# Two rings instead of one: separate buffers for modulation tiles and mixer weights

## The chip, the cores and the metric

The kernel runs on one core of a Trainium2 chip. The metric is the device time of one execution in microseconds; lower is better. The core has a matrix engine (PE), a vector engine (DVE), a scalar engine (ACT), a general engine (POOL), and SP, whose queue here only issues DMAs. Every engine takes its own queue strictly in order; engines meet through semaphores.

## The reference

One decoder layer, 256 tokens, width 2048, all in float32. Six modulation vectors come from the conditioning vector `c`; the token mixer sums a block-attention branch and a gated DeltaNet branch; then a SwiGLU feed-forward part.

```python
mod = silu(c) @ w_ada + b_ada                       # 2048 x 12288: 96 columns of 128
sh1, sc1, g1, sh2, sc2, g2 = split(mod, 6)
h = x * (1 + sc1) + sh1
proj = h @ w_in                                     # q,k,v | conv q,k,v | z | b,a | gate_a, gate_b
y_a = moba_attention(qa, ka, va)                    # 8 heads of 128
o = gated_delta_rule(l2norm(q), l2norm(k), v, ...)  # 16 heads, chunks of 64, triangular solve
y_b = rmsnorm(o) * silu(z)
y = (sigmoid(gate_a) * (y_a @ w_proj_moba) + sigmoid(gate_b) * (y_b @ w_proj_gdn)) @ w_out
x = layer_norm(ALPHA * x + g1 * y)
x = layer_norm(ALPHA * x + g2 * swiglu(x * (1 + sc2) + sh2))
```

## The kernel before

**Steps.** All large products run as 572 steps. A step loads one weight tile of up to 128 x 1024 float32 (512 KB, tile `raw`, SP issues its DMA, `load_w`, line 204), and splits it in two: ACT rounds it to `hi` (line 211), DVE computes the remainder `lo = raw - hi` (line 212). PE then multiplies in three passes (hi by activation hi, hi by activation lo, lo by activation hi): 24 matmuls of 256 columns a step (lines 289 to 291), or 12 of 512 columns (lines 337 to 339), or a wide form in the feed-forward part (lines 296 and 300). `hi` and `lo` have four buffers each. `run(3)` starts the load of a step three steps ahead.

**Modulation sums.** A column of `silu(c) @ w_ada` is not worked out on PE: a tile of w_ada lies with the 128 outputs of the column on the partitions, and one DVE instruction multiplies it with `cb` (silu of c, the same on all partitions) and adds along the row (`ada_sum`, line 229). In the opening 40 whole columns (1 MB each, tiles `r`) are summed. The other 56 columns are summed in halves of 512 KB, the tiles `raw_a` (DMA at line 240): 80 halves in the mixer and 32 in the feed-forward part. A sum leaves two rows in a listing of the queue, the multiply-and-reduce and a short read of its result.

**Buffers.** In the kernel before, `raw` and `raw_a` share one ring of four buffers of 128 x 1024, in the pool `wp`: a load waits until the tile four before it has been read.

**Background work.** After the matmuls of a step, `tick()` lets four background lanes go on (`moba`, `main`, `pre`, `ada`, in this order) for a budget of 1.8 us a step. The lanes are written as generators that yield the cost of what they did. The lane `ada` holds the modulation sums; after each sum it rests for `pace["gap"]` steps. The order in which instructions then stand in each engine's queue is set by a scheduler of the framework, with its own estimates: it can pull an instruction ahead of where the code has it. So a number of steps in `pace` is not the distance in the queue.

**Stages.** Steps 0 to 99 are the opening (first modulation vectors, first columns of w_in); 100 to 131 the attention's and the DeltaNet's q, k, v; 132 to 179 gate_a and w_proj_moba; 180 to 211 z; 212 to 243 gate_b; 244 to 275 w_proj_gdn; 276 to 307 w_out; from 308 the feed-forward part (176 steps in, 88 out).

**Block inverse.** For each of two groups of eight heads (b = 0, 1) the DeltaNet lane inverts blocks of 32 x 32 on DVE (`Ub`), copies the transpose to `mt` (line 669), and sends both through DRAM (`ubd`, POOL, lines 670 and 671) back into the tiles `UU` and `TT` (line 678). PE multiplies with `TT` into `ps` (line 691), DVE scales that to `z` (lines 700, 712), and so on; these chains stand in the same queues as the steps. In the kernel after most of these lines stand 7 higher, and 8 to 14 higher from about line 860 on.

Of the kernel before, what the change touches and what calls it, by code (L numbers as in the profile page):

```python
# [10 lines left out]
F32 = mybir.dt.float32  # L11
# [7 lines left out]
P = 128  # L19
D = 2048  # L20
S = 256
KT = D // P
# [70 lines left out]
def layer(ctx, tc, a, out):  # L93
# [57 lines left out]
    hold = {x: 0 for x in bg}  # L151
    pace = {"all": 1.8, "gap": 1, "debt": 0.0}
    done = set()
# [12 lines left out]
    def tick():  # L166
        for x in hold:
            hold[x] = max(0, hold[x] - 1)
        pace["debt"] = min(pace["debt"] + pace["all"], 2 * pace["all"])
        while pace["debt"] > 0:  # L170
            for lane in ("moba", "main", "pre", "ada"):
                c = advance(lane) if hold[lane] == 0 else None
                if c is None:
                    continue
                if c < 0:
                    hold[lane] = -c
                    continue
                pace["debt"] -= c
                if lane == "ada":
                    hold[lane] = pace["gap"]  # L180
                break
            else:
                return
# [13 lines left out]
    def until(flag):  # L197
        while flag not in done:
            yield rest()

    def load_w(w, k0, kn, c0, cn):
        raw = wp.tile([P, 1024], F32, tag="raw", name="raw", bufs=4)
        v = raw[:, :kn * cn].rearrange("p (k n) -> p k n", n=cn)
        dma.dma_start(raw[:, :kn * cn], w.tile(k0, kn, c0, cn))
        return v
# [27 lines left out]
    def ada_sums(order, ahead):  # L233
        todo = [(col, half) for col in order for half in range(2)]
        held = []
        for n in range(len(todo) + ahead):
            if n < len(todo):
                col, half = todo[n]
                raw = wp.tile([P, 1024], F32, tag="raw", name="raw_a", bufs=4)
                dma.dma_start(raw, w_ada.tile(8 * half, 8, col * P, P, by_column=True))  # L240
                held.append((col, half, raw))
            if n >= ahead:
                ada_sum(*held.pop(0), 2)
                yield 1.35
# [615 lines left out]

    def begin():
        ya = perm.tile([P, 2, MH, S], F32R, tag="s2", name="ya")
        for x in range(2):
# [7 lines left out]
    cur = {}  # L871
# [113 lines left out]
    for j in range(4, 8):  # L985
        ws_unit(ybT, w_pg, 256 * j, KT, merge(j))

    def bcast_row(v, dst):
        ps = pt.tile([P, 512], F32, tag="tp", name="tpr")
        t_.transpose(ps[:KT, :P], adac[:, 16 * v:16 * v + 16], ident)  # L990
        rw = wp.tile([KT, P], F32, tag="acc", name="rw", bufs=2)
        v_.tensor_copy(rw, ps[:KT, :P])
# [14 lines left out]
    def resid(ps, c0, cn, gb, base, dst, st, n):  # L1007
        cc = slice(c0, c0 + cn)
        for h in range(2):
            t = wp.tile([P, 512], F32, tag="acc", name="rt", bufs=2)[:, :cn]  # L1010
            v_.tensor_tensor(t, ps[h], gb[:, cc], op=OP.mult)
# [47 lines left out]

    def ffn_begin():  # L1060
        halves = [perm.tile([P, 8, 2, S], F32R, tag=tag, name="h2") for tag in ("s0", "s1")]
        cur["h2"] = halves
# [16 lines left out]
    def norm2(g):  # L1079
        r, mv, rs = cur["r"], cur["mv"], cur["rs"]  # L1080
        for f in range(4 * g, 4 * g + 4, 2):
# [4 lines left out]
            tp = pt.tile([P, 2, S], F32, tag="tp", name="tp")  # L1086
            hf = wp.tile([P, 2, S], F32, tag="acc", name="hf2", bufs=2)
            for i in range(2):
# [51 lines left out]
    def ln1_affine():  # L1140
        r = cur["r"]
        for n in range(4):
            cc = slice(512 * n, 512 * n + 512)
            for v, op in (("ln1_g", OP.mult), ("ln1_b", OP.add)):
                lg = wp.tile([P, 512], F32, tag="acc", name="lg", bufs=2)
                dma.dma_start(lg, a[v][0, cc].partition_broadcast(P))
# [4 lines left out]
    def ffn_more():  # L1151
# [3 lines left out]
        bg["ada"].append(ada_sums(range(5 * KT, 6 * KT), 1))  # L1155
        pace["gap"] = 4

# [86 lines left out]
```

## Time and profile before

| | |
|---|---|
| median of 3 runs (lowest, highest) | 1789.39 us (1779.66, 1791.91) |
| the profiled execution: its time, its span | 1785.36 us, 1783.6 us |
| PE busy | 1686.6 us (95%) |
| DVE busy | 1249.9 us (70%) |
| ACT busy | 815.2 us (46%) |
| mean granted clock of PE | 0.983 |

PE is busy 95% of the span. A busy share is an average over stages: the rows below show the stages apart.

### The profile page before, as it was taken

The page shows a single profiled execution, that of the slowest core. Times are in us where ns is not written, and L with a number is a line of the kernel's source. Part 1 is how long each engine was busy: PE and PEld are TensorE (multiplying, and loading weights), DVE is VectorE, ACT ScalarE, POOL GpSimd, SP SyncE. Part 2 cuts the span into 40 slices and gives each one's busy share as a digit, 9 for nine tenths or more (in the row PEclk, how much of TensorE's full clock was granted, in tenths as well). Part 3 has the DMA queues.
Part 4 walks back from the last instruction along what each step waited for, and adds up shares of the span by engine and source line. Part 5 has one row for each costly group of instructions (what it writes and reads, how often), then busy time and mean ns, then how long its engine had stood idle before and what let it go on. Part 6 is the DMA issues. An engine that isn't in the chain of part 4 may idle for free.

```text
span 1783.6 us, 28261 instructions
## 1 busy us (share of the span) xinstructions
PE 1686.6 (95%) x11149; PEld 1537.1 (86%) x11149; DVE 1249.9 (70%) x1786; ACT 815.2 (46%) x1118; POOL 49.9 (3%) x68
## 2 busy tenths in 40 slices
PE   3899999999989999899999899999999999999995
PEld 3899999979989788889998899888888888888895
DVE  6899988888856787657875677676666655455454
ACT  3544445667433445336344344544444444433342
POOL 0000000110100001000000000000000000000001
PEclk9999999999999999999999999999999999999998
DMA  9999887666677577876876647777777755765652
GB/s 356 331 339 353 345 310 227 199 196 189 205 238 238 186 237 247 271 239 206 296 265 222 191 129 245 251 252 239 238 246 232 242 193 192 258 197 188 197 185 82
DMA packets 115158, 421.56 MB, mean 236 GB/s; under 512 B 13456, under 2 KB 14384, under 8 KB 109392
## 3 DMA queue, kind: packets, MB, share of 16 engines
q1 hardware_dynamic: 110016, 402.21, 66.7%
q0 software_dynamic: 5008, 17.53, 3.7%
q8 instruction: 88, 1.44, 0.3%
q14 instruction: 46, 0.38, 0.1%
HBM read 412.27 MB, written 7.42 MB: 235 GB/s over the span
## 4 chain that ended last, share of the span: by engine, by line
PE 41%; issue 15%; DMA 8%; DVE 5%; ACT 1%; POOL 0%; POOLq 0%; DVEq 0%; ACTq 0%
PE mm L296 16%; PE mm L300 8%; DMA raw_a<-in_w_ada 4%; DVE lo L212 3%; PE mm L290 3%; PE mm L291 3%; PE mm L289 3%; PE mm L339 2%; PE mm L338 2%; PE mm L337 2%; DMA raw<-in_w_proj_gdn 2%; DMA raw<-in_w_in 1%; ACT hi L211 1%; PE ps L691 1%; DMA rb<-rnd 1%
## 5 line engine op out<-in xcount | busy, mean ns | idle before, releaser
L211 ACT CAST hi<-raw 128x1024 fp32r<-128x1024 f32 (+2 forms) x572 | 582.0, 1020 | 768.7 <-PE mm L339 210.7
L212 DVE TENSOR_TENSOR lo<-raw,hi 128x1024 fp32r<-128x1024 f32 (+2 forms) x572 | 672.8, 1183 | 286.1 <-ACT hi L211 282.1
L289 PE MATMUL mm<-s,hi 128*128 128x256 f32 x1184 | 338.9, 286 | 4.9 <-ACT hi L211 4.7
L291 PE MATMUL mm<-s,lo 128*128 128x256 f32 x1184 | 333.3, 283 | 6.3 <-DVE lo L212 6.2
L290 PE MATMUL mm<-s,hi 128*128 128x256 f32 x1184 | 332.5, 281 | 0.0
L296 PE MATMUL mm<-h,hi 128*128 128x512 f32 x1280 | 319.0, 391 | 0.0
L296 PEld LDWEIGHTS mm<-h,hi 128*128 128x128 f32 x1280 | 228.8, 188 | 39.5
L289 PEld LDWEIGHTS mm<-s,hi 128*128 128x128 f32 x1184 | 225.0, 190 | 10.8 <-ACT hi L211 7.5
L291 PEld LDWEIGHTS mm<-s,lo 128*128 128x128 f32 x1184 | 224.2, 190 | 9.4 <-DVE lo L212 8.5
L290 PEld LDWEIGHTS mm<-s,hi 128*128 128x128 f32 x1184 | 224.8, 190 | 0.4
L300 PEld LDWEIGHTS mm<-h,lo 128*128 128x128 f32 x1280 | 171.1, 188 | 13.2
L300 PE MATMUL mm<-h,lo 128*128 128x256 f32 x1280 | 174.1, 278 | 0.0
L337 PE MATMUL mm<-hi,ach 128*128 128x512 f32 (+1 forms) x440 | 152.6, 347 | 0.0
L338 PE MATMUL mm<-lo,ach 128*128 128x512 f32 (+1 forms) x440 | 152.5, 347 | 0.0
L339 PE MATMUL mm<-hi,acl 128*128 128x512 f32 (+1 forms) x440 | 152.5, 347 | 0.0
L229 DVE CUSTOM_DVE_ANT_0 raw_a<-raw_a,cb,cols 128x1024 f32<-128x1024 f32 x56 | 71.8, 1283 | 77.9 <-DMA raw_a<-in_w_ada 77.9
L229 DVE CUSTOM_DVE_ANT_0 raw_a<-raw_a,cb,ada_half 128x1024 f32<-128x1024 f32 x56 | 71.8, 1283 | 64.8 <-DMA raw_a<-in_w_ada 64.8
L229 DVE CUSTOM_DVE_ANT_0 r<-r,cb,cols 128x2048 f32<-128x2048 f32 x40 | 93.7, 2347 | 14.1 <-DMA r<-in_w_ada 14.1
L337 PEld LDWEIGHTS mm<-hi,ach 128*128 128x128 f32 x440 | 83.3, 189 | 10.4
L339 PEld LDWEIGHTS mm<-hi,acl 128*128 128x128 f32 x440 | 83.3, 189 | 10.4
L338 PEld LDWEIGHTS mm<-lo,ach 128*128 128x128 f32 x440 | 83.3, 189 | 10.1
L338 PE MATMUL mm<-lo,s 128*128 128x512 f32 x192 | 77.0, 401 | 2.2 <-DVE lo L212 2.2
(288 smaller groups left out, 2383.2 us busy)
## 6 DMA issues: line engine op xcount, KB each, us to landing
raw<-in_w_ffn_in SPq DMA_DIRECT2D x176, 512.0 KB, 4.3
raw<-in_w_in SPq DMA_DIRECT2D x168, 512.0 KB, 4.4
raw_a<-in_w_ada SPq DMA_DIRECT2D x112, 512.0 KB, 4.5
raw<-in_w_ffn_out SPq DMA_DIRECT2D x88, 512.0 KB, 4.3
r<-in_w_ada SPq DMA_DIRECT2D x40, 1024.0 KB, 7.6
raw<-in_w_proj_gdn SPq DMA_DIRECT2D x32, 512.0 KB, 4.5
raw<-in_w_out SPq DMA_DIRECT2D x32, 512.0 KB, 4.2
raw<-in_w_in SPq DMA_DIRECT2D x40, 384.0 KB, 5.8
```

Of the source, the lines that this page charges most:

```text
L211: s_.copy(hi, raw)
L212: v_.tensor_tensor(lo, raw, hi.bitcast(F32), op=OP.subtract)
L229: v_.tensor_tensor_reduce(out=raw, in0=raw, in1=cb[:, n * part:n * part + n], scale=1.0, scalar=cols[:, col:col + 1] if first else h, op0= ...
L289: t_.matmul(o, hi[:, i, c], ah, start=(first and i == 0 and t == 0), stop=False)
L290: t_.matmul(o, hi[:, i, c], al, start=False, stop=False)
L291: t_.matmul(o, lo[:, i, c], ah, start=False, stop=(last and i == kn - 1 and t == 1))
L296: t_.matmul(box[t].rearrange("p (u i) -> p u i", u=2), hi[:, i, t * P:(t + 1) * P], both[k0 + i], start=(first and i == 0), stop=False)
L300: t_.matmul(box[t][:, :S], lo[:, i, t * P:(t + 1) * P], both[k0 + i][:, 0, :], start=False, stop=(last and i == kn - 1))
L337: t_.matmul(box[h], xh, hi[:, i, :], start=start, stop=False)
L338: t_.matmul(box[h], xh, lo[:, i, :], start=False, stop=False)
L339: t_.matmul(box[h], xl, hi[:, i, :], start=False, stop=stop)
L691: t_.matmul(ps[:lt.shape[1], n, :], lt, rt, start=True, stop=True)
```

## The change

The diff does four things. The ring of four becomes a ring of three (`raw`) and a ring of two (`raw_a`). `load_w` takes the ring of two for two of every five weight tiles (`turn["n"] % 5 in (1, 3)`) while `turn["both"]` holds, which is in the opening and from the start of the feed-forward part; in the mixer (from `begin()` to `ffn_begin()`) weights use only the ring of three, and the ring of two holds modulation tiles alone. The rest of lane `ada` after a sum becomes 2 steps while the lanes `main` or `pre` have work, 1 otherwise, 4 in the feed-forward part as before. And small tiles (`rw`, `rt`, `hf2`, `lg`) move from pool `wp` to other pools, which makes room for the fifth buffer.

```diff
--- before.py
+++ after.py
@@ -149,7 +149,7 @@
 
     bg = {"moba": [], "main": [], "pre": [], "ada": []}
     hold = {x: 0 for x in bg}
-    pace = {"all": 1.8, "gap": 1, "debt": 0.0}
+    pace = {"all": 1.8, "gap": 2, "free": 1, "debt": 0.0}
     done = set()
 
     def advance(lane):
@@ -177,7 +177,7 @@
                     continue
                 pace["debt"] -= c
                 if lane == "ada":
-                    hold[lane] = pace["gap"]
+                    hold[lane] = pace["gap" if bg["main"] or bg["pre"] else "free"]
                 break
             else:
                 return
@@ -198,8 +198,15 @@
         while flag not in done:
             yield rest()
 
+    turn = {"n": 0, "both": True}
+
+    def raw_a(nm):
+        return wp.tile([P, 1024], F32, tag="raw_a", name=nm, bufs=2)
+
     def load_w(w, k0, kn, c0, cn):
-        raw = wp.tile([P, 1024], F32, tag="raw", name="raw", bufs=4)
+        turn["n"] += 1
+        second = turn["both"] and turn["n"] % 5 in (1, 3)
+        raw = raw_a("raw2") if second else wp.tile([P, 1024], F32, tag="raw", name="raw", bufs=3)
         v = raw[:, :kn * cn].rearrange("p (k n) -> p k n", n=cn)
         dma.dma_start(raw[:, :kn * cn], w.tile(k0, kn, c0, cn))
         return v
@@ -236,7 +243,7 @@
         for n in range(len(todo) + ahead):
             if n < len(todo):
                 col, half = todo[n]
-                raw = wp.tile([P, 1024], F32, tag="raw", name="raw_a", bufs=4)
+                raw = raw_a("raw_a")
                 dma.dma_start(raw, w_ada.tile(8 * half, 8, col * P, P, by_column=True))
                 held.append((col, half, raw))
             if n >= ahead:
@@ -859,6 +866,7 @@
             yield 0.7
 
     def begin():
+        turn["both"] = False
         ya = perm.tile([P, 2, MH, S], F32R, tag="s2", name="ya")
         for x in range(2):
             ya_ops[x].extend(ya[:, x, k, :] for k in range(MH))
@@ -985,10 +993,15 @@
     for j in range(4, 8):
         ws_unit(ybT, w_pg, 256 * j, KT, merge(j))
 
+    def acc(nm, shape):
+        if "k3" in cur:
+            return cur["k3"].tile(shape, F32, tag="acc", name=nm, bufs=2)
+        return c2(nm, shape)
+
     def bcast_row(v, dst):
         ps = pt.tile([P, 512], F32, tag="tp", name="tpr")
         t_.transpose(ps[:KT, :P], adac[:, 16 * v:16 * v + 16], ident)
-        rw = wp.tile([KT, P], F32, tag="acc", name="rw", bufs=2)
+        rw = acc("rw", [KT, P])
         v_.tensor_copy(rw, ps[:KT, :P])
         rd = dr.tile([KT, P], F32, name=f"rd{v}")
         sdma.dma_start(rd, rw)
@@ -1007,7 +1020,7 @@
     def resid(ps, c0, cn, gb, base, dst, st, n):
         cc = slice(c0, c0 + cn)
         for h in range(2):
-            t = wp.tile([P, 512], F32, tag="acc", name="rt", bufs=2)[:, :cn]
+            t = acc("rt", [P, 512])[:, :cn]
             v_.tensor_tensor(t, ps[h], gb[:, cc], op=OP.mult)
             v_.scalar_tensor_tensor(dst[:, h, cc], base[:, h, :], ALPHA, t, op0=OP.mult, op1=OP.add)
             v_.bn_stats(st[:, h, n, :], dst[:, h, cc])
@@ -1058,6 +1071,7 @@
     pss, h2 = [], []
 
     def ffn_begin():
+        turn["both"] = True
         halves = [perm.tile([P, 8, 2, S], F32R, tag=tag, name="h2") for tag in ("s0", "s1")]
         cur["h2"] = halves
         for k in range(KT):
@@ -1084,7 +1098,7 @@
                 tc.keep_in_program_order(v_.tensor_scalar(r[:, h, cc], r[:, h, cc], mv[:, h, 0:1], rs[:, h],
                                                           op0=OP.subtract, op1=OP.mult))
             tp = pt.tile([P, 2, S], F32, tag="tp", name="tp")
-            hf = wp.tile([P, 2, S], F32, tag="acc", name="hf2", bufs=2)
+            hf = acc("hf2", [P, 2, S])
             for i in range(2):
                 for h in range(2):
                     t_.transpose(tp[:, i, h * P:(h + 1) * P], r[:, h, (f + i) * P:(f + i + 1) * P], ident)
@@ -1142,7 +1156,7 @@
         for n in range(4):
             cc = slice(512 * n, 512 * n + 512)
             for v, op in (("ln1_g", OP.mult), ("ln1_b", OP.add)):
-                lg = wp.tile([P, 512], F32, tag="acc", name="lg", bufs=2)
+                lg = acc("lg", [P, 512])
                 dma.dma_start(lg, a[v][0, cc].partition_broadcast(P))
                 for h in range(2):
                     v_.tensor_tensor(r[:, h, cc], r[:, h, cc], lg, op=op)
@@ -1153,7 +1167,7 @@
         act(1, pairs_of(pss[2]), pairs_of(pss[3]))
         bg["main"].append(ln1_affine())
         bg["ada"].append(ada_sums(range(5 * KT, 6 * KT), 1))
-        pace["gap"] = 4
+        pace["gap"] = pace["free"] = 4
 
     do(ffn_more)
```

The scheduler changes the order of the queues with it. Counted against the `lo` of the weight steps, the 80 sums of the mixer stand in the queue of DVE as follows. Before: 10 in steps 100 to 159, 24 in 160 to 215, 46 in 216 to 275. After: 26, 54 and none. In steps 170 to 179 there were 10 and are 20.

SP's queue in the stage of gate_a and w_proj_moba, before: a modulation tile and a weight tile take turns.

```order
L204 DMA raw<-in_w_in 128x1024
L240 DMA raw_a<-in_w_ada 128x1024
L204 DMA raw<-in_w_in 128x1024
L240 DMA raw_a<-in_w_ada 128x1024
L204 DMA raw<-in_w_in 128x1024
L240 DMA raw_a<-in_w_ada 128x1024
L204 DMA raw<-in_w_in 128x1024
L240 DMA raw_a<-in_w_ada 128x1024
L204 DMA raw<-in_w_proj_moba 128x1024
L240 DMA raw_a<-in_w_ada 128x1024
```

The same place after.

```order
L211 DMA raw<-in_w_proj_moba 128x1024 x2
L247 DMA raw_a<-in_w_ada 128x1024 x2
L211 DMA raw<-in_w_in 128x1024
L247 DMA raw_a<-in_w_ada 128x1024 x7
L211 DMA raw<-in_w_in 128x1024
L247 DMA raw_a<-in_w_ada 128x1024
L211 DMA raw<-in_w_in 128x1024 x2
L247 DMA raw_a<-in_w_ada 128x1024 x2
L211 DMA raw<-in_w_proj_moba 128x1024
L247 DMA raw_a<-in_w_ada 128x1024
L211 DMA raw<-in_w_proj_moba 128x1024
```

Seven loads of modulation tiles now stand in a row between two loads of weights.

DVE's queue at the first head group's chain, before (`lo` is a weight step; `z` and `bv` are the chain's; the `ISA` rows are sums).

```order
L712 TENSOR_TENSOR z<-ps_5657,bcs 64x256
L212 TENSOR_TENSOR lo<-raw,hi 128x1024
L712 TENSOR_TENSOR z<-ps_5664,bcs 64x256
L212 TENSOR_TENSOR lo<-raw,hi 128x1024
L229 ISA raw_a,ada_half<-raw_a,cb,cols 128x1024
L229 ISA ada_half 128x1
L229 ISA raw_a,adac<-raw_a,cb,ada_half 128x1024
L229 ISA adac 128x1
L730 SCALAR_TENSOR_TENSOR bv_3442<-pr_5759,nb,bv_3442 128x128 x2
L212 TENSOR_TENSOR lo<-raw,hi 128x1024
L730 SCALAR_TENSOR_TENSOR bv_3442<-pr_5769,nb,bv_3442 128x128 x2
```

The same place after; the row ahead of the first one here is a `lo`.

```order
L236 ISA raw_a,ada_half<-raw_a,cb,cols 128x1024
L236 ISA ada_half 128x1
L236 ISA raw_a,adac<-raw_a,cb,ada_half 128x1024
L236 ISA adac 128x1
L719 TENSOR_TENSOR z<-ps_5588,bcs 64x256
L719 TENSOR_TENSOR z<-ps_5595,bcs 64x256
L236 ISA raw_a,ada_half<-raw_a,cb,cols 128x1024
L236 ISA ada_half 128x1
L236 ISA raw_a,adac<-raw_a,cb,ada_half 128x1024
L236 ISA adac 128x1
L737 SCALAR_TENSOR_TENSOR bv_3439<-pr_5682,nb,bv_3439 128x128 x2
L737 SCALAR_TENSOR_TENSOR bv_3439<-pr_5692,nb,bv_3439 128x128 x2
```

Before, two sums stand among the chain's rows and three `lo`; after, four sums and no `lo`, and three more sums follow the last row ahead of the next `lo`, so that seven stand between two `lo`.

DVE's queue behind the copy `mt` of the second block inverse (b = 1), before; the first row is the copy.

```order
L669 COPY mt<-Ub 64x1024
L212 TENSOR_TENSOR lo<-raw,hi 128x1024
L780 TENSOR_SCALAR oss<-oss 128x16
L347 TENSOR_SCALAR oe<-oss,epsc 128x16
L212 TENSOR_TENSOR lo<-raw,hi 128x1024
L349 RECIPROCAL or<-or 128x16
L350 TENSOR_TENSOR ors<-or 128x16
L351 TENSOR_TENSOR ors<-ors,oe 128x16
L352 TENSOR_SCALAR ors<-ors 128x16
L353 TENSOR_TENSOR ors<-or,ors 128x16
L212 TENSOR_TENSOR lo<-raw,hi 128x1024
L787 SCALAR_TENSOR_TENSOR yb_6586<-bv_3442,ors,yb_6586 128x128 x16
```

After; the copy stands right ahead of the first row here, and the last row is the chain's first multiply, which reads what PE made with `TT`.

```order
L787 TENSOR_SCALAR oss<-oss 128x16
L354 TENSOR_SCALAR oe<-oss,epsc 128x16
L219 TENSOR_TENSOR lo<-raw,hi 128x1024
L356 RECIPROCAL or<-or 128x16
L357 TENSOR_TENSOR ors<-or 128x16
L358 TENSOR_TENSOR ors<-ors,oe 128x16
L359 TENSOR_SCALAR ors<-ors 128x16
L360 TENSOR_TENSOR ors<-or,ors 128x16
L219 TENSOR_TENSOR lo<-raw,hi 128x1024
L794 SCALAR_TENSOR_TENSOR yb_6562<-bv_3439,ors,yb_6562 128x128 x16
L219 TENSOR_TENSOR lo<-raw,hi 128x1024 x2
L707 TENSOR_TENSOR z<-ps_7371,bcs 128x512
```

After, four `lo` lie between the copy and that multiply; before, 16 did. For the first block inverse it is 4 where it was 8.

SP's queue in the stage of w_proj_gdn, before.

```order
L240 DMA raw_a<-in_w_ada 128x1024
L204 DMA raw<-in_w_proj_gdn 128x1024
L240 DMA raw_a<-in_w_ada 128x1024
L204 DMA raw<-in_w_proj_gdn 128x1024
L240 DMA raw_a<-in_w_ada 128x1024
L204 DMA raw<-in_w_proj_gdn 128x1024
L240 DMA raw_a<-in_w_ada 128x1024
L204 DMA raw<-in_w_proj_gdn 128x1024
L240 DMA raw_a<-in_w_ada 128x1024
```

After.

```order
L211 DMA raw<-in_w_in 128x1024 x25
L211 DMA raw<-in_w_proj_gdn 128x1024 x6
L1058 DMA xs<-in_x 128x2x512
L211 DMA raw<-in_w_proj_gdn 128x1024 x26
L211 DMA raw<-in_w_out 128x1024 x5
```

Here the modulation tiles are gone; nothing but weights and one load of x is left.

## Rows read from the trace of the kernel before

**Rows 1.** Windows by stage: length, busy us of each engine, PEclk, DMA share, GB/s.
```profile
23.30:273.40 250.10, 237.90 (x1912) 227.60 (x1913) 228.72 (x275) 115.40 (x161) 5.26 (x9) 0.99 0.90 336
273.40:481.10 207.70, 198.89 (x1407) 184.65 (x1406) 177.48 (x375) 130.77 (x199) 16.34 (x26) 0.98 0.63 198
481.10:701.50 220.40, 207.79 (x1296) 184.47 (x1295) 151.49 (x265) 92.66 (x151) 18.30 (x22) 0.97 0.72 228
701.50:923.10 221.60, 208.45 (x1703) 203.82 (x1702) 157.84 (x224) 95.44 (x151) 0.88 (x1) 0.98 0.78 257
...
1060.00:1518.00 458.00, 457.91 (x2711) 405.38 (x2710) 305.08 (x374) 221.79 (x293) 0.00 (x0) 1.00 0.71 232
```

**Rows 2.** Windows, the modulation sums alone (DVE), over the three mixer stages.
```profile
273.40:481.10 207.70, 12.78 (x10) 0.98 0.63 198
481.10:701.60 220.50, 32.03 (x25) 0.97 0.72 228
701.60:923.10 221.50, 57.74 (x46) 0.98 0.78 257
```

**Rows 3.** Windows inside the mixer, columns as in Rows 1.
```profile
273.40:300.40 27.00, 27.00 (x234) 26.90 (x233) 20.63 (x35) 16.01 (x26) 0.00 (x0) 1.00 0.65 205
417.10:452.30 35.20, 33.18 (x273) 32.30 (x273) 29.43 (x67) 28.41 (x41) 1.67 (x2) 1.00 0.58 183
452.30:481.10 28.80, 27.16 (x231) 26.72 (x230) 27.61 (x53) 10.76 (x11) 1.46 (x2) 1.00 0.57 181
481.10:534.60 53.50, 46.32 (x368) 45.30 (x367) 28.71 (x44) 18.29 (x30) 7.99 (x10) 0.94 0.82 249
534.60:578.20 43.60, 43.39 (x365) 42.18 (x364) 28.27 (x38) 15.95 (x26) 0.56 (x1) 1.00 0.74 238
578.20:621.70 43.50, 40.47 (x214) 33.71 (x213) 30.95 (x63) 19.33 (x28) 1.63 (x3) 0.96 0.58 183
621.70:701.50 79.80, 77.61 (x356) 63.28 (x355) 63.55 (x123) 39.09 (x69) 8.12 (x8) 0.98 0.72 234
786.80:790.20 3.40, 3.02 (x14) 3.02 (x15) 3.40 (x6) 1.58 (x3) 0.00 (x0) 0.50 0.83 249
```

**Rows 4.** The modulation tile raw_a in the mixer, 273.4 to 923.1 us.
```profile
L229 DVE CUSTOM_DVE_ANT_0 raw_a<-raw_a,cb,cols x40: 1272/1283/1287, 297.0 to 893.9; 128x1024 f32<-128x1024 f32 x40
...
  DMA raw_a<-in_w_ada: 76.7, 44
...
DMA to landing us min/median/max: 3.4/4.6/8.0
```

**Rows 5.** Waits of SP's DMA queue, mixer: us, times, longest.
```profile
SPq L204 <- DVE lo L212: 209.6, 96, 9.3
...
SPq L204 <- DVE adac L229: 48.7, 19, 9.2
...
SPq L204 <- DVE ada_half L229: 46.0, 18, 9.4
```

**Rows 6.** Waits of PE, 701.6 to 923.1 us: us, times, longest.
```profile
PE ps L691 <- DVE z L700: 7.5, 2, 4.2
```

**Rows 7.** Timeline of DVE in the output projection: start, us, line, idle before.
```profile
940.13 1.23 DVE L212 TENSOR_TENSOR lo<-raw,hi 128x1024 fp32r<-128x1024 f32 x1 [1.50 <-ACT hi L211]
942.81 1.23 DVE L212 TENSOR_TENSOR lo<-raw,hi 128x1024 fp32r<-128x1024 f32 x1 [1.45 <-ACT hi L211]
```

**Rows 8.** Timeline of POOL at the second block inverse (head group b = 1).
```profile
682.02 1.10 POOL L671 DMA_DIRECT2D ubd<-mt  x1 [4.14 <-issue]
...
687.59 0.89 POOL L678 DMA_DIRECT2D TT<-ubd  x1 [3.58 <-DMA ubd<-mt]
```

**Rows 9.** The tile mt there: the transposing copy.
```profile
L669 DVE COPY mt<-Ub x1: 1137/1137/1137, 676.0 to 676.0; 64x1024 f32<-64x1024 f32 x1
```

**Rows 10.** The tile TT over the mixer.
```profile
DMA to landing us min/median/max: 6.1/7.1/8.1
```

## The prediction

> **What bounds the kernel now.** I read the windows by stage first, since the share of PE over the whole span hides where it waits. In the opening (23.3 to 273.4 us) PE works 237.90 of 250.10 us, and DVE 228.72, and the DMA share is 0.90: three resources near their limit. In the three mixer stages PE works 198.89 of 207.70, 207.79 of 220.40 and 208.45 of 221.60 us, which leaves it idle for 8.8 + 12.6 + 13.2 = 34.6 us in all; from 1060 to 1518 us it works 457.91 of 458.00 [rows 1]. So PE is the bound nearly everywhere, and what a change of order can give back lies in those 34.6 us, and in the clock: the granted clock is 0.98, 0.97 and 0.98 in the three stages, because some short stretches behind a pause of PE run at half of it, as 786.8 to 790.2 us at 0.50 [rows 1, 3]. Three per cent of 220 us are 6.6 us, two per cent of 429 us 8.6, so 15 us at most.
>
> Second, who makes PE wait. DVE has room on average: 177.48, 151.49 and 157.84 us busy in those stages [rows 1]. But it sat idle for 76.7 us in 44 places until a modulation tile had landed, and every weight step behind such a place waits with it. The transfer takes 4.6 us in the median, the sum 1283 ns [rows 4]. SP's queue in turn could not issue a weight load for 209.6 us until a `lo` had freed a buffer, and for 48.7 + 46.0 = 94.7 us until a sum had [rows 5]: that is the shared ring. Where no sum is about, as in the output projection, one `lo` follows another by 942.81 - 940.13 = 2.68 us, with DVE idle for 1.45 us of it [rows 7]: PE's rate. Those DVE waits are long against 34.6 us of idle PE, so most of them are hidden already by the four buffers of `hi` and `lo`.
>
> **The change part by part.** The sums go, by the order of DVE's queue, from 10, 24 and 46 in the three mixer stages to 26, 54 and none (the trace of before shows the same 10, about 25 and about 46 [rows 2]). No work is added or removed; 80 sums stay 80, about 103 us of DVE.
>
> *Steps 100 to 159, 16 sums more.* Sixteen times 1.283 is 20.5 us of DVE. By ten steps: 6 more in the first ten, where DVE has 27.00 - 20.63 = 6.4 us of idle time, for 7.7 us of work: 1.3 too much. Five more in steps 140 to 149, 35.20 - 29.43 = 5.8 us idle for 6.4: 0.6 too much. Six more in steps 150 to 159, where DVE is busy for 27.61 of 28.80 us: 7.7 us into 1.2, so 6.5 too much [rows 3]. The rest nearly cancels. The sum of the excess is 8.4 us. Below, it could be nothing, if PE lives from the `lo` tiles already there; above, all 20.5 count, if no idle time is usable. I take **+8**, near the fill of the idle time, because in the last ten steps there is none to fill.
>
> *Steps 160 to 179: 18 sums and 28.* The excess lies in steps 170 to 179, 20 sums where 10 were. That stretch (534.6 to 578.2) is PE's, 43.39 busy of 43.60 us, and DVE works 28.27 us [rows 3], so ten more sums (12.8 us) would fit by busy time: 41.1 us, a cost of nothing. But with two buffers a sum can't come more often than (4.6 landing + 1.28 sum + some 0.3 for the issue) / 2 = 3.1 us; twenty are 62 us, which is 18 more than the stretch has. And SP is in order: with seven `raw_a` loads in a row in its queue, it stands at each until the sum two before has ended, and weight loads queue behind it, so three `raw` tiles and the split ones are all that PE has. Against that, seven of the sums stand beside the DeltaNet chain of the first group, in which PE has its own 60 matmuls to do. Between 0 and +18 I take the middle, **+9**: ten more sums at the mean wait of before, 76.7 / 80 = 0.96 us each [rows 4], come out there too. Steps 160 to 169 (46.32 of 53.50 busy [rows 3]) keep their 8 sums; there the copy `mt` of the first inverse comes only four steps ahead of its use, but seven microseconds of PE are idle already, and I put 0 (-8 to +8).
>
> *Steps 180 to 215, 15 sums more.* 19.2 us of DVE, and it has 43.50 - 30.95 + 79.80 - 63.55 = 28.8 us idle up to 701.5 [rows 3]. They come evenly, at about seven in ten steps. The excess is nothing by busy time and 19 at most; **+3**, since pairs of sums ahead of a `lo` delay a step by up to 2.6 us and only some of that reaches PE.
>
> *Steps 216 to 275, 46 sums less.* The gain: SP issues nothing but weights here, 58 us of DVE go, and PE can run at its own rate. What it can give is bounded by the idle PE, 13.2 us, and two per cent of clock, 4.4 us: -17.6 at most. PE's longest waits there are for the chain's `z`, 7.5 us in two places [rows 6]; sums stood ahead of those `z` in DVE's queue, so a part of them should go. The cost is a new wait: the second block inverse. Its copy `mt` (1.14 us from 676.0 [rows 9]) was done at 677.1, `ubd` was issued at 682.02, `TT` at 687.59 [rows 8], and a `TT` lands 7.1 us after its issue [rows 10]: 694.7, so 17.6 us from the copy's end until PE can start. Sixteen `lo` covered that before; four do now. Four steps at 2.68 us [rows 7] are 10.7: a wait of 6.9 us if PE is four steps behind DVE, and 14.9 if it is only one behind. What waits behind `z` in DVE's queue then are the next `lo`, but those four ahead give PE work once `TT` has come. I take a gain of 17 and a cost of 8, **-9**; the ends are -17.6 (`TT` is covered) and +8 (15 of wait, 7 gained).
>
> *Opening.* There the five buffers serve weights alone (the tiles `r` have their own ring), one more than before. With DMA at 0.90 and DVE at 91% [rows 1] deeper prefetch finds little: **-2** (-6 to +3).
>
> *From 923 us on.* The feed-forward part has its sums spaced by 4 steps before and after; PE fills it [rows 1]. The moved small tiles add no instruction. **-1** for two weight tiles fetched early (-3 to +3).
>
> Sum: -2 + 8 + 9 + 0 + 3 - 9 - 1 = **+9 us**, on the profiled execution's 1785.36: 1794. The median of the runs is 1789.39, 4 us above that execution, and the lowest 1779.66; I leave the sum where it is, on the profiled one. A measurement of this kernel can tell about 1% (18 us) from no change, so this is "no change".
>
> **A rule of the Trainium skill that speaks against the change.** What the row shows: POOL sat for 4.14 us between two DMA issues of the block inverse with nothing that it waited for ("issue") [rows 8]. The Trainium skill ("SBUF — State Buffer", section "SBUF: two separate sides") says that a DMA issued by POOL has its descriptors written by POOL's cores, and that they can't write while DVE runs an operation that holds the port pair the two share; it names copies, and is silent on the multiply-and-reduce. If sums hold it, denser sums would hold up the DMAs of the DeltaNet lane. Those are about twelve issues in steps 140 to 216, each held by at most one sum, 12 x 1.283 = 15 us [rows 4]. The row fits this and does not show it.
>
> **Rivals.**
> *Faster: the waits for the shared ring go.* For it: 94.7 us in which weight loads waited for a sum [rows 5], and 34.6 us of idle PE next to them; with rings apart a weight load never waits for a sum's buffer. If two thirds of the idle time and 10 of the 15 us of clock come back: -23 - 10 + 2 = about 1755. Against it: in one queue a load behind a waiting `raw_a` waits all the same, and the chain's own waits stay.
> *Slower: the two-buffer ring sets the pace.* In steps 160 to 215 the sums alone need 54 x 3.1 = 167 of the 220 us, and in steps 170 to 179 more than there is. If SP, stopped at `raw_a`, starves PE each time: +18 there, +10 in the rest of that stage, +12 in steps 100 to 159, +8 for the two inverses, gain -14: +34, 1819. It decides once the landing takes more than about twice PE's step, 2 x 2.68 = 5.4 us; it ranged to 8.0 [rows 4].
> *The port.* By that rule, all 15 on the chain: 1809.
> *It doesn't do what it says.* "Every second step" is not in the queue: seven sums in a row stand there. If the scheduler's moves also cancel otherwise, nothing changes: 1786 to 1790, inside the forecast.
>
> **How the numbers follow.** Forecast (with the cancelling case) 0.55, faster 0.17, slower 0.21, port 0.05, others 0.02. The forecast's own range by the ends of its terms, not all on one side, is 1772 to 1812. To leave out no more than two in ten I reach half into both rivals: 1766 to 1818. Faster by over 1% (below 1771.5): 0.19; slower by over 1% (above 1807.3): 0.27; within: 0.54.
>
> **What would show it.** In the profile after: no modulation sum behind step 215; there PE near 97% of the time, with one new wait of 7 to 15 us on `TT`. In steps 170 to 179, PE idle by some 9 us, DVE waiting for `raw_a` and SP's weight loads waiting behind it. DVE without idle time in steps 150 to 159. Wrong it would be if weight loads never wait behind a sum's (then faster), or if the two inverses' waits add to full length (then slower).

## The result and the profile after

The kernel after takes 1799.05 us in the median of 9 runs (1796.53 to 1805.07), the kernel before 1785.96 us (1779.66 to 1791.91, 9 runs). The ratio is 1.0076, with a 95% interval of 1.0062 to 1.0091: slower by 0.8%, within the 1% forecast as "no change" and within the range. The interval lies wholly above 1, so the loss is real, and a measurement resolves this kernel far better than the 1% that the prediction gave it. The forecast was +9 us on the profiled execution, and +13.7 were found there (span 1783.6 to 1797.3 us).

The windows of the kernel after, cut at the first `lo` of steps 100, 160, 170, 180, 216 and 276 as [rows 1, 3] are (the third row is steps 150 to 159 alone, the last two are stretches at low clock): length, busy us of PE, PE's loads, DVE, ACT, POOL, then PEclk, DMA share, GB/s.

```profile
23.30:270.70 247.40, 235.47 (x1898) 225.48 (x1899) 228.24 (x275) 114.61 (x160) 5.24 (x9) 0.99 0.93 343
270.70:486.40 215.70, 200.00 (x1428) 185.81 (x1427) 191.04 (x393) 129.73 (x198) 14.86 (x24) 0.98 0.72 230
454.90:486.40 31.50, 30.06 (x257) 29.86 (x256) 31.11 (x55) 10.99 (x11) 0.00 (x0) 1.00 0.79 272
486.40:533.10 46.70, 36.96 (x286) 36.38 (x284) 28.35 (x53) 14.93 (x17) 8.29 (x10) 0.88 0.76 247
533.10:598.40 65.30, 57.33 (x447) 55.25 (x448) 45.93 (x73) 20.24 (x40) 1.44 (x2) 0.92 0.83 273
598.40:719.20 120.80, 118.12 (x570) 94.76 (x570) 105.28 (x193) 53.36 (x64) 4.52 (x6) 0.99 0.83 281
719.20:935.90 216.70, 204.46 (x1689) 201.25 (x1689) 111.24 (x155) 100.95 (x182) 6.07 (x6) 0.98 0.51 164
529.00:537.50 8.50, 1.11 (x5) 1.11 (x6) 3.25 (x5) 1.04 (x1) 0.56 (x1) 0.50 1.01 344
737.00:741.00 4.00, 2.49 (x11) 2.49 (x12) 0.38 (x1) 0.83 (x1) 0.00 (x0) 0.50 0.97 335
```

Against [rows 1, 3] the opening ends 2.7 us earlier (270.7 for 273.4). Steps 100 to 159 take 215.7 us for 207.7: +8.0, with DVE's busy time up from 177.48 to 191.04, and in steps 150 to 159 DVE has 0.4 us of idle time left. Steps 160 to 169 take 46.7 for 53.5, steps 170 to 179 take 65.3 for 43.6: together +14.9. PE idles for 17.7 of these 112.0 us, for 7.4 of 97.1 before: 10.3 of the 14.9. The other 4.6 are longer busy time for the same 733 matmuls, at a granted clock of 0.88 and 0.92 where it was 0.94 and 1.00. Steps 180 to 215 take 120.8 for 123.3 (-2.5), steps 216 to 275 take 216.7 for 221.5 (-4.8). Behind step 276 the two agree within a microsecond. These lengths come from one profiled execution of each kernel, and executions of one kernel lie up to 9 to 12 us apart, so a stage's difference of 2 or 3 us says little.

The sums, in the same windows as [rows 2] (DVE's busy time on `raw_a`):

```profile
273.40:486.40 213.00, 34.51 (x27) 0.98 0.72 230
486.40:719.20 232.80, 67.64 (x53) 0.95 0.81 272
719.20:935.90 216.70, 0.00 (x0) 0.98 0.51 164
```

What PE waited for (us in total, times, longest). In steps 100 to 159 its waits for `w` and `pT`, tiles of the background lanes, before:

```profile
PE ps_c L520 <- DVE w L516: 2.3, 1, 2.3
PE poa L856 <- ACT pT L851: 1.0, 1, 1.0
```

After:

```profile
PE poa L863 <- ACT pT L858: 6.8, 3, 4.2
PE ps_c L527 <- DVE w L523: 5.9, 1, 5.9
```

From 480 to 920 us the longest waits are now for `TT`:

```profile
PE ps L698 <- DMA TT<-ubd: 19.7, 2, 11.1
```

There are two, 11.1 and 8.6 us. In steps 160 to 179 before, nearly all of PE's waiting was this:

```profile
PE ps L691 <- DVE z L712: 4.0, 1, 4.0
PE tp L587 <- DVE n L583: 3.2, 1, 3.2
```

The same place after (486 to 600 us):

```profile
PE ps L698 <- DMA TT<-ubd: 11.1, 1, 11.1
PE pv L742 <- DVE bv L737: 2.9, 2, 2.3
PE mm L298 <- DVE lo L219: 1.8, 1, 1.8
PE po L746 <- DVE bv L737: 1.7, 1, 1.7
```

The timeline of POOL at the two inverses answers to [rows 8]:

```profile
521.09 1.11 POOL L678 DMA_DIRECT2D ubd<-mt  x1 [6.65 <-DVE kq L604]
...
527.76 0.91 POOL L685 DMA_DIRECT2D TT<-ubd  x1 [3.99 <-DMA ubd<-mt]
...
726.77 1.10 POOL L678 DMA_DIRECT2D ubd<-mt  x1 [4.08 <-issue]
...
732.35 0.89 POOL L685 DMA_DIRECT2D TT<-ubd  x1 [3.60 <-DMA ubd<-mt]
```

The second one has the rhythm of before, 5.6 us between the two issues; only the cover is gone. The first is worse, and DVE's queue shows why: the copy `mt` was ready when `Ub` ended at 511.07, but in the new order it stands behind a `kq` that waits for another DMA.

```profile
510.87 0.20 DVE L673 TENSOR_TENSOR Ub<-Ub,tm 64x31 f32<-64x31 f32 x1
517.88 0.69 DVE L604 TENSOR_TENSOR kq<-kq,rb 128x512 f32<-128x512 f32 x1 [6.81 <-DMA rb<-rnd]
518.49 1.13 DVE L676 COPY mt<-Ub 64x1024 f32<-64x1024 f32 x1
```

For the sums of steps 160 to 179 (486 to 600 us) DVE's idle time ahead of them and the landing times answer to [rows 4]. Before, the idle time in these steps was 29.5 us in 16 places, so DVE stands no longer for its sums than it did, although there are ten more.

```profile
  DMA raw_a<-in_w_ada: 21.9, 14
...
DMA to landing us min/median/max: 3.5/4.6/11.6
```

And SP's queue in the same stretch: the seven loads of `raw_a` in a row take 17.34 us, since each waits for the sum two before, and the next weight load stands behind them. PE hardly felt it: from 536.4 to 592.2 us its longest idle time is 0.69 us.

```profile
542.06 0.33 SPq L211 DMA_DIRECT2D raw<-in_w_in  x1
543.40 17.34 SPq L247 DMA_DIRECT2D raw_a<-in_w_ada  x7
561.55 0.33 SPq L211 DMA_DIRECT2D raw<-in_w_in  x1
```

### The profile page after: what moved, and what is told of

It reads as the page before. It is cut to its first block, busy times and chain, and to the rows that moved or that the text cites. A ratio compares the mean times of both kernels' runs of the same rounds, so it can differ in the third digit from the quotient of the medians.

```text
span 1797.3 us, 28226 instructions
## 1 busy us (share of the span) xinstructions
PE 1686.7 (94%) x11149; PEld 1536.4 (85%) x11149; DVE 1244.0 (69%) x1786; ACT 814.2 (45%) x1118; POOL 49.6 (3%) x68
## 4 chain that ended last, share of the span: by engine, by line
PE 43%; issue 15%; DMA 3%; DVE 2%; ACT 1%; POOL 0%; POOLq 0%; SPq 0%; ACTq 0%
PE mm L303 16%; PE mm L307 8%; PE mm L297 4%; PE mm L298 4%; PE mm L296 4%; PE mm L344 2%; PE mm L345 2%; PE mm L346 2%; DMA raw_a<-in_w_ada 1%; DVE lo L219 1%; PE ps L698 1%; DMA Mb<-mbd 0%; DMA TT<-ubd 0%; PE tp L1104 0%; ACT hi L218 0%
## 5 line engine op out<-in xcount | busy, mean ns | idle before, releaser
L296 PEld LDWEIGHTS mm<-s,hi 128*128 128x128 f32 x1184 | 226.2, 191 | 12.2 <-ACT hi L218 8.8
L344 PEld LDWEIGHTS mm<-hi,ach 128*128 128x128 f32 x440 | 83.4, 189 | 10.3
```

Source lines behind the costliest of these rows:

```text
L296: t_.matmul(o, hi[:, i, c], ah, start=(first and i == 0 and t == 0), stop=False)
L344: t_.matmul(box[h], xh, hi[:, i, :], start=start, stop=False)
```

## Experiments

Theory A: the ring of two lets the scheduler run the sums ahead; they crowd DVE in steps 100 to 159, and push the block inverse so close to its use that PE waits for `TT`. Rival B: the ring of two itself, with SP's strict order, holds every step where sums are dense. A second rival is the pacing. All runs are compared with the kernel before on the same chip. The chain of inverse and use can move work from one stage into another, so a stage's length alone does not tell what was lost there. Stage lengths below are cut at the first `lo` of steps 100, 160, 216 and 276:

| kernel | ratio to before (95%) | steps 100-159 | 160-215 | 216-275 | from 276 |
|---|---|---|---|---|---|
| before | 1 | 207.7 | 220.4 | 221.5 | 860.5 |
| after | 1.0076 (1.0062 to 1.0091) | 215.7 | 232.8 | 216.7 | 861.4 |
| e1: old pacing | 1.0014 (1.0000 to 1.0028) | 217.4 | 226.2 | 205.8 | 860.5 |
| e2: new pacing alone | 1.0131 (1.0100 to 1.0161) | 218.8 | 209.2 | 230.7 | 870.4 |
| e3: one ring of five | 0.9969 (0.9942 to 0.9996) | 213.9 | 214.6 | 211.3 | 860.2 |
| e4: all half sums pinned | 1.0361 (1.0341 to 1.0381) | 205.6 | 210.4 | 215.7 | 942.0 |
| e5: other source of `TT` | 1.0101 (1.0073 to 1.0129) | 218.4 | 234.3 | 215.1 | 861.2 |
| e6: second lead long | 1.0069 (1.0052 to 1.0086) | 217.1 | 227.8 | 211.9 | 861.4 |
| e7: pinned in the mixer, old pacing | 0.9910 (0.9895 to 0.9924) | 205.8 | 215.4 | 211.2 | 860.6 |
| e8: pinned, new pacing | 0.9954 (0.9934 to 0.9974) | 209.2 | 209.1 | 217.7 | 871.1 |
| e9: shared ring of four, pinned | 1.0095 (1.0072 to 1.0117) | 207.9 | 228.5 | 224.6 | 861.1 |
| e10: shared ring of five, pinned | 0.9927 (0.9904 to 0.9950) | 204.7 | 219.1 | 214.1 | 861.4 |
| e11: e7 with short leads | 0.9983 (0.9967 to 1.0000) | 205.4 | 244.4 | 200.9 | 854.8 |
| e12: after with long leads | 1.0052 (1.0030 to 1.0074) | 218.5 | 234.4 | 208.9 | 861.3 |

Three rows part the change into its pieces, one at a time. The fifth buffer, with the small tiles moved (before to e3), gives 0.31%; splitting the five into three and two (e3 to e1) costs 0.45%; the new pacing (e1 to after) costs 0.62%. That is -5.5, +8 and +11 us. The new pacing also costs in the two other pairs that differ by it alone: 1.31% with the ring of four (before to e2) and 0.44% with pinned sums (e7 to e8).

**e1, the rings with the old pacing.**

```diff
-    pace = {"all": 1.8, "gap": 2, "free": 1, "debt": 0.0}
+    pace = {"all": 1.8, "gap": 1, "free": 1, "debt": 0.0}
```

> The changed kernel with the old pacing (a rest of 1 step after each sum). Theory A (the two rings let the sums run ahead; they crowd DVE in steps 100 to 159 and push the block inverse so near to its use that PE waits for TT): the sums still stand 28, 52 and 0 in the three mixer stages, so 1797 to 1802 us, as the changed kernel. If the pacing were the cause of the loss: 1780 to 1788.

1785.06 us, 1.0014. The sums stand as expected (28, 52, none), and yet most of the loss is gone: the expectation of theory A failed, that of the pacing was met. PE's waits of this kernel hold only one wait for `TT`:

```profile
PE ps L698 <- DMA TT<-ubd: 10.5, 1, 10.5
```

The second inverse has a lead of 8 weight steps here, not 4. So here the pacing hardly changes where the sums stand, but shifts what else the scheduler places. Steps 100 to 159 keep their loss (217.4).

**e2, the pacing with the old ring.**

> The kernel before, one shared ring of four, with the new pacing alone. The sums move back (8, 16, 35 in the mixer stages and 21 in steps 270 to 291), the inverse keeps 9 and 16 weight steps of lead. Theory A: no wait for TT, fewer sums in the crowded stretches, and in steps 270 to 291 a sum (1.28 us) fits into the 1.45 us that DVE is idle per step: 1776 to 1786. If the pacing causes the loss: 1793 or more.

1804.13 us, 1.0131: slower, against theory A's figure. The figure for a loss by the pacing was met, as in e1. The sums do move back. The loss is 11 us in steps 100 to 159, 9 in 216 to 275 and 10 behind, and 11 are gained in 160 to 215. The expectation of no wait for `TT` failed too:

```profile
PE ps L691 <- DMA TT<-ubd: 5.9, 1, 5.9
```

That is at the second inverse, whose lead is 16 weight steps. The lead counts `lo` in DVE's queue up to the chain's first multiply there; PE had come to its own first multiply with `TT` 10 us after the copy, while DVE's came 52 us after it. So a long lead by this count does not rule the wait out. A window over steps 276 to 307, with sums in it:

```profile
931.40:1030.20 98.80, 91.72 (x454) 73.39 (x454) 72.98 (x92) 35.63 (x35) 0.00 (x0) 0.99 0.81 278
```

By their first `lo` these steps took 88.5 us before (923.1 to 1011.6). DVE is idle for 25.8 of these 98.8 us, and yet they are 10 us longer: that a sum fits into DVE's idle time did not make it free. e8 looks at such steps more closely.

**e3, one shared ring of five.**

```diff
-        raw = wp.tile([P, 1024], F32, tag="raw", name="raw", bufs=4)
+        raw = wp.tile([P, 1024], F32, tag="raw", name="raw", bufs=5)
...
-                raw = wp.tile([P, 1024], F32, tag="raw", name="raw_a", bufs=4)
+                raw = wp.tile([P, 1024], F32, tag="raw", name="raw_a", bufs=5)
```

> The kernel before with one shared ring of five instead of four (and the small tiles moved), old pacing. The order of the sums stays that of before. If the fifth buffer is what helps the opening: 2 to 5 us less there, 1781 to 1784. If separate rings matter there: 1786 as before. No theory expects a loss.

1775.86 us, 0.9969: below both figures. The opening gives 2 us and steps 216 to 275 give 10; a loss of 6 in steps 100 to 159 and a gain of 6 in 160 to 215 cancel. A fifth buffer, without separation, is a small gain.

**e4, pinned sums.**

```diff
-        v_.tensor_tensor_reduce(out=raw, in0=raw, ...
+        ins = v_.tensor_tensor_reduce(out=raw, in0=raw, ...
...
+        if parts == 2:
+            tc.keep_in_program_order(ins)
```

The call puts an instruction behind what stands ahead of it on its engine in the order of the code.

> The changed kernel with every half-column sum pinned behind what stands ahead of it in the program's own order on DVE. Rings of three and two stay; the sums stand 9, 28 and 43 as before the change, the inverse has 8 and 15 weight steps of lead again. Theory A: the loss goes, 1780 to 1787. Rival B (the ring of two itself sets the pace, weight loads stand behind modulation loads in SP's queue): the loss stays wherever sums stand, above all in steps 170 to 179 (11 sums) and 216 to 269, 1795 or more.

1845.27 us, 1.0361. The counts in the expectation are wrong: in the trace 6, 17 and 57 sums stand in steps 100 to 159, 160 to 219 and 220 to 299. The loss lies where it says nothing on either theory: behind step 276 (942.0 for 860.5 us), 12 us in the output projection and 69 in the feed-forward part. There PE waits 44.4 us, in 21 places, for the `hi` of a weight tile; how the pins bring that about was not followed up. In steps 100 to 215 it is the fastest of these four. e7 and e8 drop the pins in the feed-forward part.

**e5, no round trip of the inverse.**

```diff
-                sdma.dma_start(dst, ubd[w][8 * hh:8 * hh + 8, :P, :].rearrange("u c i -> c u i"))
+                sdma.dma_start(dst, mbd[b][8 * hh:8 * hh + 8, :P, :].rearrange("u c i -> c u i"))
```

> The changed kernel, but UU and TT are loaded from the other DRAM array (the one that holds the blocks before inversion), which is complete long before; so the values of the DeltaNet chain are others, all work and the order of sums and weight steps stay. PE no longer waits for the round trip of the inverse. Theory A (the inverse's short lead is the larger part of the loss; PE waited 19.7 us for TT, and then ran at a granted clock of 0.5 for a while): 1770 to 1782. Rival B (the ring of two and SP's order hold the steps where sums are dense, the waits for TT only lie beside that): 1792 to 1799.

1799.90 us. It settles nothing: the wait was not removed, as PE's waits show (two, 10.8 and 6.6 us):

```profile
PE ps L698 <- DMA TT<-mbd: 17.4, 2, 10.8
```

`TT` takes the buffer of an earlier tile of the same three-buffer ring (`Mb`, `Ub`, `mt`, `UU`, `TT`), so its load still stands behind the inverse.

**e6, a longer second lead.**

```diff
-            yield rest(((9, 4), (20, 6))[b][hh])
+            yield rest(((14, 4), (34, 6))[b][hh])
```

> The changed kernel with longer rests between the inverse and its use (14 and 34 steps for 9 and 20). In the order only the second group's lead grows, from 4 weight steps to 23; the first stays at 4. Theory A: the second wait for TT (8.6 us) and the slow clock behind it go, the first (11.1 us) stays: 1786 to 1791. Rival B: no change, 1797 to 1800. A third possibility: the later chain runs into the next need for its result, and the gain is given back there.

1794.52 us, 1.0069; the profiled span is 1790.5 for 1797.3. The second wait is gone, the first stays (10.9 us). Neither theory's figure was met. By the ratios, 1.0069 and 1.0076 with intervals that overlap, a gain over the kernel after is not shown. PE has new waits instead, 3.4 us for a `lo` behind step 220 among them; that the rest is given back where the chain now ends is argued and not shown.

**e7, separate rings, sums held in program order in the mixer.** As e4, old pacing, and with

```diff
-        if parts == 2:
+        if parts == 2 and (bg["main"] or bg["pre"]) and not turn["both"]:
             tc.keep_in_program_order(ins)
```

> Separate rings as in the change, the old pacing, and in the mixer every sum that is issued while the lanes main or pre have work is pinned behind what stands ahead of it on DVE; in the feed-forward part nothing is pinned. The sums stand 9, 28 and 43 as before the change, none behind step 269; leads 8 and 15. Theory A: nothing is left of the loss, and up to step 260 the 30 us that the pinned kernel was ahead of before should mostly stay: 1755 to 1775. Rival B: 1785 or more.

1766.08 us, 0.9910: the fastest kernel, 1.7% below the changed one. Same rings, same buffers, same work as e1; only the sums may not run ahead. Its windows, steps 100 to 159, 160 to 215 and 216 to 275:

```profile
270.60:476.40 205.80, 197.43 (x1420) 183.67 (x1419) 177.08 (x373) 131.33 (x199) 18.03 (x27) 0.98 0.62 199
476.40:691.80 215.40, 206.78 (x1300) 183.82 (x1299) 150.16 (x265) 92.80 (x150) 16.63 (x21) 0.98 0.72 232
691.80:903.00 211.20, 205.99 (x1704) 202.72 (x1704) 159.54 (x226) 94.76 (x151) 0.88 (x1) 0.98 0.79 272
```

Against the kernel after these are 9.9, 17.4 and 5.5 us less; against e1, from which the pins alone part it, 11.6 and 10.8 less and 5.4 more. No wait for the DMA of `TT` is left. The pins put the sums back and, with them, the leads of the inverse (8 and 15), so this run shows that the order makes the loss, not which part of the order.

**e8, the same with the new pacing.**

> The same with the pacing of the change (a rest of 2 steps): 6, 17 and 35 sums in the mixer stages and 22 in steps 270 to 291, all in w_proj_gdn's end and w_out. It differs from the pinned kernel by the feed-forward part alone, which cost that one 69 us: 1845 - 69 = 1776, so 1770 to 1782; of the 30 us gained up to step 260 some 24 are given back in steps 260 to 300.

1776.62 us, 0.9954, as expected. It loses where a sum comes with every step: steps 280 to 289, with 12 sums, take 42.2 us for 27.2. SP's waits there (918 to 961 us), and the window:

```profile
SPq L249 <- DVE ada_half L236: 16.0, 6, 4.1
SPq L249 <- DVE adac L236: 14.7, 6, 3.7
```

```profile
918.50:960.70 42.20, 33.05 (x121) 23.01 (x120) 30.48 (x40) 10.48 (x11) 0.00 (x0) 0.92 0.90 313
```

SP stands for 30.7 us at modulation loads with the weight loads behind: B's mechanism. And the DMA share is 0.90 at 313 GB/s: one weight tile and one modulation tile a step are 1.05 MB, which at that rate take 3.35 us, more than PE's 2.68 [rows 7]. Which of the two sets the step of 4.2 us was not separated.

**e9 and e10, the pins with a shared ring of four, and of five.** The edit of e7 in the kernel before, and in e3.

> The kernel before, one shared ring of four, old pacing, with the pins of e7 (mixer sums issued while main or pre have work). The sums stand 9, 28 and 43 as in e7 and as before. It tells whether e7's gain is the rings' or the pins'. Rings: 1779 to 1786, as before. Pins (a sum no longer ahead of older DVE work): 1764 to 1772.

> The shared ring of five with the same pins and pacing. If the fifth buffer and not the separation makes e7's gain: 1764 to 1770, as e7. If weights must not share with sums: 1775 or more, near the ring of five without pins (1776).

1799.77 us (1.0095) and 1770.34 us (0.9927). e9 missed both of its figures; e10 lies beside the one for the fifth buffer. With four buffers the pins cost; with five, shared, they gain, and e10 and e7 can't be told apart by their intervals. So e7's gain comes from the fifth buffer together with the pins; that separation by itself helps is not shown. e9 is not a clean test of the pins: its second inverse has a lead of 5 weight steps where before had 16, and PE waits once for the DMA of `TT`, which it did not before:

```profile
PE ps L694 <- DMA TT<-ubd: 4.6, 1, 4.6
```

The pins change the ratio by -1.0% with split rings (e1, e7), -0.4% with a shared five (e3, e10) and +1.0% with a shared four.

**e11, e7 with short leads.**

```diff
-            yield rest(((9, 4), (20, 6))[b][hh])
+            yield rest(((5, 4), (9, 6))[b][hh])
```

> e7 with shorter rests between the inverse and its use (5 and 9 steps for 9 and 20): leads of 4 and 4 weight steps, as the changed kernel has, with the sums spread as before. Theory A: PE waits for TT twice, 7 to 15 us each, with a slow clock behind: 12 to 25 us above e7, 1778 to 1791. If the lead matters little (the chain's time is only moved and is got back behind): 1766 to 1771.

1779.03 us, 0.9983 for 0.9910: 13 us, in the expected interval, with the sums spread as before. PE's waits:

```profile
PE ps L700 <- DMA TT<-ubd: 11.7, 2, 6.4
```

So short leads by themselves cost 13 us: the lead matters, as theory A has it. Its windows, the same stages as those of e7:

```profile
270.70:476.10 205.40, 198.06 (x1420) 184.83 (x1420) 176.72 (x374) 131.49 (x199) 18.08 (x27) 0.98 0.62 200
476.10:720.50 244.40, 227.26 (x1402) 201.54 (x1401) 152.06 (x270) 100.46 (x168) 17.32 (x22) 0.94 0.62 206
720.50:921.40 200.90, 196.36 (x1642) 193.44 (x1642) 158.40 (x221) 89.95 (x135) 1.10 (x2) 1.00 0.84 292
```

That 11.6 us of waiting and 13 us of time lie close is not a rule of one for one. PE's idle time in the three stages rose by 6.8 us only (29.0 for 22.2), as waits of e7 went, and PE worked longer at a granted clock of 0.94 in steps 160 to 215, for 0.98. The chain, starting earlier, took 102 matmuls into that stage and left 10 and 6 us less to the stages behind.

**e12, the kernel after with long leads.**

```diff
-            yield rest(((9, 4), (20, 6))[b][hh])
+            yield rest(((24, 4), (30, 6))[b][hh])
```

> The changed kernel with rests of 24 and 30 steps between inverse and use: leads of 12 and 22 weight steps instead of 4 and 4, the sums as far ahead as in the change (27, 53, none). Theory A: no wait for TT is left (19.7 us, and some slow clock behind each), so 1774 to 1784; what then still stands above e7 (1766) is the crowding of DVE by sums, some 10 us in steps 100 to 159. Rival B (dense sums on a ring of two hold the steps by themselves): 1790 to 1799. Given back later (the chain's end now comes later and holds what needs it): 1785 to 1792.

1791.29 us, 1.0052: by the ratios 4 us below the kernel after, with intervals that overlap. Theory A's figure was missed; the time lies in B's range and in that of the third reading. No wait for the DMA of `TT` is left, but the time came back as other things:

```profile
271.30:489.80 218.50, 203.06 (x1425) 189.37 (x1424) 191.13 (x393) 129.84 (x198) 14.86 (x24) 0.95 0.69 227
489.80:724.20 234.40, 208.82 (x1272) 182.13 (x1271) 173.56 (x302) 97.96 (x154) 14.27 (x18) 0.96 0.81 273
724.20:933.10 208.90, 205.49 (x1719) 202.37 (x1718) 118.23 (x172) 94.17 (x150) 6.06 (x6) 1.00 0.50 167
```

In steps 160 to 215 PE works 208.82 of 234.40 us, no better than after (212.41 of 232.80). What it waits for in 480 to 600 us is DVE:

```profile
PE mm L298 <- DVE lo L219: 7.2, 4, 3.0
PE pv L742 <- DVE bv L737: 5.6, 1, 5.6
PE ps L698 <- DVE z L707: 3.7, 1, 3.7
```

So with 53 sums there the chain's own DVE steps (`bv`, `z`) and `lo` stand behind sums that wait for their tile. Covering `TT` uncovers that.

## Why the prediction held, and where its terms were off

The total was near, the terms less so: the errors of three of them, +5.9, -5.5 and +4.2 us, in part cancel, and that is luck. The terms as written add up to +8, not +9.

**Opening, -2:** measured -2.7.

**Steps 100 to 159, +8:** measured +8.0. The sum is right and the stretches are not, so its closeness is luck too: 1.3, 0.6 and 6.5 us were forecast for steps 100 to 109, 140 to 149 and 150 to 159, and by the `lo` starts they are +6.6, -3.0 and +2.8, with +1.6, -3.9 and +3.9 between. PE's idle time rose by 6.9 of the 8.0 us (15.7 for 8.8), and its longest waits are for `w` and `pT`, not for a weight tile. That the order costs some 10 us here is shown: the five kernels with these rings whose sums stand 27 or 28 here (after, e1, e5, e6, e12) take 215.7 to 218.5 us, the four with pinned sums (e4, e7, e8, e11) 205.4 to 209.2. The number of sums is not the whole of it: e2 and e3 have 8 and 11 and take 218.8 and 213.9. There PE works longer, 207.6 and 205.1 us for 198.9, at granted clocks of 0.95 and 0.96.

**Steps 160 to 179, +9 and 0:** measured +14.9, the term that was mis-sized. I had put 0 on the first inverse, because PE was idle there anyway. The trace shows a wait of 11.1 us, with a granted clock of 0.50 from 529.0 to 537.5 us, in place of 7.2 us for `z` and `n`. The inverse's copy came 7 us late, behind a `kq`. The missed step is the order of DVE's queue at `mt`: I counted the four `lo` behind the copy, not what stood ahead of it.

The +9 was for dense sums that starve PE of weight tiles through SP's queue. SP did stand, and DVE did wait, but PE waited for a weight tile for 1.8 us only. Its other waits are 4.6 us for the chain's `bv`, which stands behind sums that wait for their tile:

```profile
590.14 1.29 DVE L236 CUSTOM_DVE_ANT_0 raw_a<-raw_a,cb,ada_half 128x1024 f32<-128x1024 f32 x1 [3.96 <-DMA raw_a<-in_w_ada]
...
593.81 0.61 DVE L737 SCALAR_TENSOR_TENSOR bv<-pr,nb,bv 128x128 f32<-128x128 f32 x2
```

So the sign "PE idle by some 9 us in steps 170 to 179" came true (8.0) for other reasons: 3.3 us are the end of the wait for `TT`, and the rest is waiting for `bv`.

**Steps 180 to 215, +3:** measured -2.5, below the nothing that was its lower end. The sums were miscounted there: the prediction's own counts give 20 more (6 and 26), the traces 18 (7 and 25), not 15. The larger number cost nothing either.

**Steps 216 to 275, -9:** measured -4.8, from a wait for `TT` of 8.6 us (8 expected) and a gain of about 13 in place of 17. The 17 counted on all of PE's idle time and on the clock; beside `TT` 3.6 us of idle time remain, and the granted clock is 0.98 as before. So PE works 94% of the time there, not near 97. e1 and e7, without that wait, reach 205.8 and 211.2.

**From 923 us on, -1:** +0.9.

**The pacing** had no term at all. Its 0.62% (e1 to after) is most of the measured 0.76%. Of these 11 us, 8.6 would be the second wait for `TT` by the traces, since e1 has only the first; but e6 takes that wait away with the new pacing kept, and its ratio moves by 0.07%. So how the pacing makes its loss stays open.

**The rivals.** The faster one failed for the changed order. Where the order is kept, e7 is 0.9% below before, about half of what it named; its mechanism, that weight loads no longer share with sums, is not shown by that, since e10 with one shared ring comes as low. The slower one, a pace set by the ring of two, was too large as priced: +14.9 in steps 160 to 179, with 1.8 us of it as a wait of PE for a weight tile, and nothing in 180 to 215. "It doesn't do what it says" was right of the queue, and wrong in that the pacing has no part. The rule on POOL's DMAs (the Trainium skill, "SBUF — State Buffer", "SBUF: two separate sides") got no support, and the row that I took to fit it does not: no sum runs in the idle 4.14 us of [rows 8] (677.9 to 682.0 us), nor in the 4.08 us ahead of the second `ubd` after (722.7 to 726.8). No run here tests it further.

**What stays open:** how much of the fifth buffer's gain needs separate rings (e7 and e10 agree), why a shared ring of four with pins is slower than without them (e9; its wait of 4.6 us for `TT` is a part at most), how the 17 us of steps 160 to 215 between after and e7 split between the leads and dense sums, and how the pacing costs what it does.

## What to carry to other kernels

A buffer ring of its own frees a stream from waiting, and so frees a list scheduler to run it ahead; read from the order where the freed work now stands, and what it was pulled in front of. Here, with five buffers, a prefetched side stream cost least where its instructions stayed at their place and only its loads ran ahead. Take a change apart into its pieces, and run each alone: what looked like a change of rings lost more by the pacing that came with it than by the split. When two stalls overlap in one stretch, remove each alone and both together before putting a price on either: short leads cost 13 us by themselves (e11), and lengthening them beside dense sums gave some 4 us back, within the noise (e12).

## What the runs showed of the hardware

In steps 280 to 289 of e8, with 12 modulation tiles beside ten weight tiles, 313 GB/s at a DMA share of 0.90 was reached, and a step took 4.2 us where PE alone needs 2.7 [rows 7]. DVE worked 30.48 of the 42.20 us, so a side stream can lengthen a step although the engine that works on it has time left.

While the first `TT` was awaited, the DMA share was 1.01 at 344 GB/s, and this `TT` landed 8.6 us after its issue, for 7.1 in the median before [rows 10]. Landings of `raw_a` reached 11.6 us there, for 8.0 before [rows 4]. Near the end of the second wait the share was 0.97, and PE could start 6.2 us after that issue; so what a full DMA costs one transfer is not shown.

The granted clock fell to 0.50, the lower of its two levels (1.2 of 2.4 GHz), not only behind a pause of PE. In the kernel after PE worked all of the 17 us from 474 to 491 us at 1.00, and the row from 491.0 to 497.9 us then has 0.51, with PE busy throughout. In e11 it stood at 0.50 from 509.1 to 522.8 us, with PE busy all the while and for 16.83 of the 17.00 us ahead of that.
